# A hybrid SSM and attention layer on one core: x, B, C and z projected in row-block pairs by seven products, in a stage of their own ahead of attention

## The chip, the cores and the metric

One core of one Trainium2 chip. The metric is the device time of one execution in microseconds (us), the median of several runs. A core has five engines that run side by side, each in the order of its own instruction stream: TensorE (PE, matrix products into PSUM), VectorE (DVE), ScalarE (ACT, functions by tables), GpSimd (POOL) and SyncE (SP). In this kernel nearly every transfer is queued on SP and carried out by 16 DMA engines.

## The reference

One layer of a streaming encoder for T = 1088 columns: a prompt of 1024 positions and a running stream of 64 that has 512 cached positions. D = 1024.

```python
xn = rmsnorm(x)
z, xbc, dt, q, k, v, gate_ssm, gate_att = split(xn @ w_in)   # 2048, 3072, 32, 1024, 1024, 1024, 1024, 1024
xbc = silu(causal_dwconv(xbc, width 4) + b)                   # -> x (2048), B (512), C (512)
y = ssd_scan(x, dt, B, C) + D_skip * x                        # chunks of 64, 32 heads in 4 groups
y = rmsnorm_by_group(y * silu(z))
o = rmsnorm(softmax(q1 k1) v - lam * softmax(q2 k2) v)        # 8 heads, chunk-causal, q and k normed and rotated
mix = sigmoid(gate_ssm) * (y @ w_branch_ssm) + sigmoid(gate_att) * (o @ w_branch_attn)
x = x + mix @ w_out
ha, hb = split(rmsnorm(x) @ w_up)                             # 2816 each
x = x + (silu(causal_dwconv(ha, width 3)) * hb) @ w_down
```

Everything is float32. Outputs are the layer's result, the new keys and values, the scan's state and the last rows ahead of both convolutions.

## The kernel before

**Layout and precision.** Activations lie transposed: 128 features on the partitions, positions along the columns. A feature dimension of 1024 is eight row blocks (KT = 8). Each float32 operand is split into a high and a low part of a type that TensorE takes at full rate (`hi`, `lo`); a product is three matmuls, hi by hi, hi by lo and lo by hi (`product`, L149 to L151). A projected row block of 128 features runs over three column parts, WIDE = 384, 384, 320, with 24 matmuls for each (`project`): a *step* of the generators below. `weights` loads a block of weights, ACT makes its high part (L142) and DVE its low part (L143). `acc` hands out PSUM banks in turn.

**Order of the stages.** Front norm, from which come xn in high and low parts and the values' first half; statistics of the scan (`steps`); q; values 2 and 3; the cached keys; k. Then attention with its filler, the scan with its filler, the second half of the SSM branch, the output product with the second norm, the FFN's up-projection and its down-projection.

**Filler.** The projections of x, B and C (24 row blocks, `conv_tiles`), z (16, `z_tiles`) and the two branch gates (16, `gate_tiles`) are no stage. They are one generator, `stream`, in the order of the list ORDER, 168 steps. `fill(rate)` draws so many steps of it: ATT_STEPS = 1.9 after each attention unit, SCAN_STEPS = 1.5 at each of the scan's yields. From the fifth yield of the scan on (BRANCH_AT = 4) the generator is followed by `branch_tiles`: the attention branch (24 steps) and the first half of the SSM branch (24 steps).

**Attention.** Eight heads, nine units each (128 query positions, in the order ATT_ORDER; the last block is the stream's 64). A unit (`attend`, L510 to L586) makes two score rows of up to 1024 columns in PSUM tiles `sc`, of which there are two (L535, L536); DVE takes the maximum (L540, L544); ACT the exponential (L549); DVE the reciprocal, lambda and the difference of the two softmaxes (L551 to L553); PE transposes (L564), DVE and ACT copy (L571), PE multiplies with the values (L583). `head_out` norms a head's output (L604, L609).

**Scan.** 36 chunk steps over four groups and three column parts. It reads x, B, C (`x_sc`) and z (`z_sc`) back from memory, where the filler put them, and broadcasts decays from `a_sc`.

**Convolution and silu.** The conv block's first tap and bias are an ACT instruction (L458), three taps are DVE instructions (L460). silu is made from tanh: an ACT instruction and a DVE one (L462, L431), with the factor 0.5 folded into the parameters and the group norm's scale.

**The up-projection** already uses seven products: two row blocks by two halves of the inner dimension are one 2 x 2 block matrix, the columns in two halves the other side, and seven products of block sums take the place of eight (L992 and the lines 149 to 151 over tiles of QW = 272 columns). The weights' sums are made on GpSimd, the split into parts on ACT and DVE (L841, L842), the sums of products on DVE out of PSUM; its convolution of width 3 is L1001 and L1003.

**What sets the order.** A planner orders each engine's instructions: it holds a timeline of its own, takes what is ready by it, and among that what the program has earlier; `tc.high_priority(n)` moves an instruction ahead. The program's order above is thus a priority, not the order on the engine.

Of the kernel before, what the change touches and what calls it, by code (L numbers as in the profile page):

```python
# [12 lines left out]
ALU = mybir.AluOpType  # L13
# [52 lines left out]
ORDER = (("g", (15, 14)), ("z", range(4)), ("c", group(0)), ("g", range(13, 7, -1)), ("c", group(1)), ("c", group(2)),  # L66
         ("z", range(4, 8)), ("c", group(3)), ("z", range(8, 16)), ("g", range(7, 1, -1)))

# [7 lines left out]
def hybrid_layer(ctx: ExitStack, tc: tile.TileContext, xT, prm, cst, rope, wvd, win, wbs, wba, wout, wup, wdn,  # L76
# [9 lines left out]
    def scratch(name, shape, dt=F32):  # L86
        return dram.tile(shape, dt, name=name, tag=name)

    q_st, k_st = (scratch(n, [2 * D, T]) for n in ("q_st", "k_st"))
    c_st = scratch("c_st", [2 * D, PAST])  # L90
# [30 lines left out]
    xn_pool = tc.alloc_tile_pool(name="xn", bufs=1, side="right")  # L121

    def rows_by_part(name):

        return [[xn_pool.tile([P, KT, w], R32, name=f"{name}_{u}{x}", tag=f"{u}{x}") for u in ("hi", "lo")]
                for x, (c, w) in enumerate(WIDE)]

    xn = rows_by_part("xn")
    extra, turn, ahead, quick = None, 0, AHEAD_IN, QUICK
# [23 lines left out]
    def project(block, evac):  # L153
        w_hi, w_lo = weights(block, KT, P)
        for (c, w), (hi, lo) in zip(WIDE, xn):
            ps = acc(w)
            product(ps, [(w_hi[:, k], w_lo[:, k], hi[:, k], lo[:, k]) for k in range(KT)])
            with tc.high_priority(quick or ahead):
                evac(ps, c, w)
            yield  # L160
# [74 lines left out]
    with tc.tile_pool(name="nx", bufs=1) as nx:  # L235
        S.preload_act_table_set(LN_EXP)
        c = 0
        for x, w in enumerate(NORM):
            xc = nx.tile([P, KT, max(NORM)], F32, name="xc", tag="xc", bufs=3)
            ps = stat(w)  # L240
            for k in range(KT):
                load(out=xc[:, k, :w], in_=xT[:, k, c : c + w])
                if x == 0 and k == 3:
                    load(out=con, in_=cst)
            if x == 0:
                load(out=par, in_=prm)
                for a, b, by in ((O_MIX, O_CW, -1.0), (O_CW, O_SN, 0.5), (O_SN, O_D, -0.5), (O_QN, O_FW, -1.0)):
                    V.tensor_scalar_mul(par[:, a:b], par[:, a:b], by)
            for k in range(KT):
                sq = nx.tile([P, max(NORM)], F32, name="nsq", tag="nsq", bufs=NSQ)  # L250
                if k % 2:
                    (G if x else V).tensor_tensor(out=sq[:, :w], in0=xc[:, k, :w], in1=xc[:, k, :w], op=ALU.mult)
                else:
                    act(sq[:, :w], xc[:, k, :w], AF.Square)
                PE.matmul(ps, ones, sq[:, :w], start=k == 0, stop=k == KT - 1)
            rs = nx.tile([P, max(NORM)], F32, name="nrs", tag="nrs", bufs=2)
            rstd_of(nx, rs[:, :w], ps, w, "nn", 1.0 / D, max(NORM))
            for k in range(KT):
                xr = nx.tile([P, max(NORM)], F32, name="nxr", tag="nxr", bufs=NXR)
                (G if k % 3 == 2 else V).tensor_tensor(out=xr[:, :w], in0=xc[:, k, :w], in1=rs[:, :w], op=ALU.mult)  # L260
                hi, lo = (t[:, k, c % 384 : c % 384 + w] for t in xn[c // 384])
# [6 lines left out]

    def values(f, dt=None, pools=(None, None)):
        m = 256 if dt is None else 272  # L270
        w2 = [weights(win[B_V + 2 * f - 4 + u] if dt is None else wvd[2 * f + u], 4, m, pools[u]) for u in range(2)]
        for i in range(9):
            n = min(P, T - i * P)
            ps = acc(m)[:n]
            hi, lo = (t[:, :, P * (i % 3) : P * (i % 3) + n] for t in xn[i // 3])
            product(ps, [(hi[:, k], lo[:, k],
                          w2[k // 4][0][:, k % 4], w2[k // 4][1][:, k % 4]) for k in range(KT)])
            vo = staged("vo")[:, :256]
            with tc.high_priority(quick or ahead):
# [15 lines left out]
    with tc.tile_pool(name="qk", bufs=1) as qk:  # L295
# [113 lines left out]
        heads(B_K, lambda j: col(O_KN + j), k_st, kT)  # L409
    s1.close()  # L410
    more = None, 0
    ahead = AHEAD
    extra.release()
    extra = None
    cv_pool = tc.alloc_tile_pool(name="cv", bufs=1, side="right")

# [8 lines left out]

    def z_tiles(tiles):
        for j in tiles:
            def evac(ps, c, w):
                zr = staged("zr")[:, :w]
                act(zr, ps, AF.Tanh, scale=0.5)  # L430
                V.scalar_tensor_tensor(zr, zr, 1.0, ps, ALU.add, ALU.mult)  # L431
                load(out=z_sc[P * j : P * (j + 1), c : c + w], in_=zr)

            yield from project(win[B_Z + j], evac)

    def conv_tiles(tiles):
        for f in tiles:
            tail = None

            def evac(ps, c, w):  # L440
                nonlocal tail
                n = min(w, TP - c)
                pre = cv_pool.tile([P, 387], F32, name="pre", tag="pre", bufs=2)
                cc = cv_pool.tile([P, 384], F32, name="cc", tag="cc", bufs=3)
                if tail is None:
                    G.memset(pre[:, 0:3], 0.0)
                else:
                    G.tensor_copy(pre[:, 0:3], tail)
                S.copy(pre[:, 3 : 3 + n], ps[:, :n])
                tail, m = pre[:, n : n + 3], w  # L450
                if n < w:
                    m = w + 3
                    G.tensor_copy(pre[:, n + 3 : n + 6], par[:, O_CS + 3 * f : O_CS + 3 * f + 3])
                    S.copy(pre[:, n + 6 : w + 6], ps[:, n:])
                    G.tensor_copy(conv_o[:, f, 0:3], tail)
                    G.tensor_copy(conv_o[:, f, 3:6], pre[:, w + 3 : w + 6])
                cw = lambda i: col(O_CW + 4 * f + i)
                act(cc[:, :m], pre[:, :m], AF.Identity, bias=col(O_CB + f), scale=cw(0))  # L458
                for i in range(1, 4):
                    V.scalar_tensor_tensor(cc[:, :m], pre[:, i : i + m], cw(i), cc[:, :m], ALU.mult, ALU.add)  # L460
                act(pre[:, :m], cc[:, :m], AF.Tanh)
                V.scalar_tensor_tensor(cc[:, :m], pre[:, :m], 1.0, cc[:, :m], ALU.add, ALU.mult)  # L462
                load(out=x_sc[P * f : P * (f + 1), c : c + n], in_=cc[:, :n])
                if n < w:
                    load(out=x_sc[P * f : P * (f + 1), c + n : c + w], in_=cc[:, n + 3 : m])

            yield from project(win[B_X + f], evac)

    def stream():
        for kind, which in ORDER:  # L470
            yield from {"c": conv_tiles, "z": z_tiles, "g": gate_tiles}[kind](which)
        two = [gate_tiles([j]) for j in (1, 0)]
        for _ in WIDE:
            for u in two:
                yield next(u)
# [176 lines left out]
    with (tc.tile_pool(name="sin", bufs=1) as sin, tc.tile_pool(name="sp", bufs=1) as sp,  # L652
# [77 lines left out]
        def normed(g, c, w, xs, zt, y):  # L730
# [10 lines left out]
            load(out=part(y_sc), in_=y)  # L741

        def scan():
# [40 lines left out]
        def branch_tiles():  # L784
            nonlocal bs
            cv_pool.release()
            st.release()
            bs = tc.alloc_tile_pool(name="bs", bufs=1, side="right")
# [30 lines left out]
    bs.release()  # L819
    xn_pool.release()  # L820

# [386 lines left out]
```

## Time and profile before

| | |
|---|---|
| three runs | 2530.85, 2530.01, 2529.93 us; median 2530.01 |
| the profiled execution: span | 2526.9 us, first to last instruction |
| its own time beside the runs' | the median is 3.1 us above that span |
| PE busy | 2463.0 us (97%), 16646 matmuls |
| DVE / ACT / POOL busy | 1507.9 (60%) / 1130.1 (45%) / 522.8 us (21%) |
| DMA | 378.75 MB, 150 GB/s over the span |
| mean granted TensorE clock | 0.990 of full speed |

Rough times of the stages in the profile: q, k and values until about 390 us, attention until about 1105, the scan until about 1580, the rest of the branch and the output product until about 1770, the second norm until about 1820, the up-projection until about 2235. A busy time is the sum of an engine's instructions; PE's matmuls overlap in the pipeline, so that a matmul's own duration is longer than the distance to the next one's start.

### The profile page before, as it was taken

To read this page: it belongs to the slowest core of one execution; us is meant where nothing else is said; L and a number is where in the kernel's file an instruction comes from. 1 tells how busy PE (TensorE), PEld (TensorE's weight loads), DVE (VectorE), ACT (ScalarE), POOL (GpSimd) and SP (SyncE) were. 2 spreads that over 40 slices of the span, in tenths; PEclk is the share of its full clock that TensorE was granted. 3 is DMA by queue.
4 is the path that set the end of the run, shared out by engine and by line. 5 is a ranking of instruction groups with operands and counts; after the bars stand their busy time and mean duration, and the time that the engine had idled before them with its cause. 6 is when DMAs were issued, how large, how long until landed. Compare 5 with 4: busy or idle time off the path is not lost.

```text
span 2526.9 us, 43448 instructions
## 1 busy us (share of the span) xinstructions
PE 2463.0 (97%) x16646; PEld 2385.1 (94%) x16646; DVE 1507.9 (60%) x2597; ACT 1130.1 (45%) x2426; POOL 522.8 (21%) x584
## 2 busy tenths in 40 slices
PE   8999999999999999999999998999699999999999
PEld 8999999999999999998889898998699999999999
DVE  7326255855787677447667764645876666673422
ACT  6234343644666455357655654225443333341200
POOL 3000000100111001014333230014465555530000
PEclk9999999999999999999999999999799999999999
DMA  5217258545354344255697735663122222256553
GB/s 164 77 55 272 77 202 261 153 143 158 108 150 138 112 144 118 87 198 177 204 350 233 231 126 201 189 203 109 39 82 78 77 77 78 76 193 211 174 159 112
DMA packets 248336, 378.75 MB, mean 150 GB/s; under 512 B 31776, under 2 KB 188320, under 8 KB 248000
## 3 DMA queue, kind: packets, MB, share of 16 engines
q1 hardware_dynamic: 248128, 375.97, 46.6%
q8 instruction: 131, 2.15, 0.4%
q14 instruction: 77, 0.63, 0.1%
HBM read 254.58 MB, written 121.30 MB: 149 GB/s over the span
## 4 chain that ended last, share of the span: by engine, by line
PE 71%; DMA 4%; DVE 3%; ACT 2%; issue 1%; SPq 1%; POOL 0%; ACTq 0%; DVEq 0%; POOLq 0%
PE mx L992 12%; PE mm L149 10%; PE mm L151 10%; PE mm L150 10%; PE mm L992 5%; PE mx L151 4%; PE mx L149 4%; PE mx L150 4%; PE po L583 3%; PE sc L536 1%; PE sc L535 1%; PE pt L564 1%; PE yi L698 1%; PE ye L704 1%; DMA bc<-a_sc 1%; PE stp L710 1%
## 5 line engine op out<-in xcount | busy, mean ns | idle before, releaser
L149 PE MATMUL mm<-xn_hi,w_hi 128*128 128x384 f32 (+1 forms) x1416 | 469.8, 332 | 0.9 <-DVE zr L431 0.9
L151 PE MATMUL mm<-xn_hi,w_lo 128*128 128x384 f32 (+1 forms) x1416 | 467.7, 330 | 0.4 <-DVE w_lo L143 0.4
L150 PE MATMUL mm<-xn_lo,w_hi 128*128 128x384 f32 (+1 forms) x1416 | 466.5, 329 | 0.0
L142 ACT CAST w_hi<-w_f 128x1024 fp32r<-128x1024 f32 (+2 forms) x144 | 149.3, 1037 | 308.1 <-PE mx L150 162.2
L149 PEld LDWEIGHTS mm<-xn_hi,w_hi 128*128 128x128 f32 x1416 | 266.2, 188 | 5.3 <-issue 2.0
L151 PEld LDWEIGHTS mm<-xn_hi,w_lo 128*128 128x128 f32 x1416 | 266.1, 188 | 2.9 <-issue 0.8
L150 PEld LDWEIGHTS mm<-xn_lo,w_hi 128*128 128x128 f32 x1416 | 266.2, 188 | 1.8 <-issue 0.6
L143 DVE TENSOR_TENSOR w_lo<-w_f,w_hi 128x1024 fp32r<-128x1024 f32 (+2 forms) x144 | 181.2, 1259 | 133.4 <-ACT w_hi L142 133.0
L149 PE MATMUL mm<-b_hi,w_hi 128*128 128x384 f32 (+1 forms) x448 | 148.2, 332 | 7.6 <-DVE b_g L193 4.4
L151 PE MATMUL mm<-b_hi,w_lo 128*128 128x384 f32 (+1 forms) x448 | 147.0, 328 | 0.0
L150 PE MATMUL mm<-b_lo,w_hi 128*128 128x384 f32 (+1 forms) x448 | 146.9, 328 | 0.0
L992 PE MATMUL mx<-n,wh 128*128 128x272 f32 x752 | 143.4, 289 | 1.4 <-ACT wh L841 1.4
L992 PE MATMUL mx<-m,w_hi 128*128 128x272 f32 x752 | 142.7, 288 | 0.0
L460 DVE SCALAR_TENSOR_TENSOR cc<-pre,par,cc 128x384 f32<-128x384 f32 (+1 forms) x216 | 126.6, 586 | 23.8 <-ACT cc L458 18.7
L549 ACT ACTIVATE p_t<-sc,mx 128x1024 f32<-128x1024 f32 (+5 forms) x144 | 106.1, 739 | 74.6 <-DVE mx L540 37.1
L992 PEld LDWEIGHTS mx<-n,wh 128*128 128x128 f32 x752 | 118.3, 189 | 1.7 <-ACT wh L841 1.7
L992 PEld LDWEIGHTS mx<-m,w_hi 128*128 128x128 f32 x752 | 118.1, 188 | 0.0
L1009 POOL TENSOR_TENSOR hb<-hb,cc 128x544 f32<-128x544 f32 (+2 forms) x66 | 88.4, 1353 | 115.1 <-ACT w_hi L841 95.0
L151 PE MATMUL mx<-m,w_lo 128*128 128x272 f32 (+2 forms) x366 | 111.9, 307 | 0.0
L150 PE MATMUL mx<-m,w_hi 128*128 128x272 f32 (+2 forms) x366 | 111.9, 306 | 0.0
L149 PE MATMUL mx<-m,w_hi 128*128 128x272 f32 (+2 forms) x366 | 111.8, 306 | 0.0
L992 PE MATMUL mx<-m,w_lo 128*128 128x272 f32 x376 | 108.4, 288 | 0.0
(339 smaller groups left out, 6595.4 us busy)
## 6 DMA issues: line engine op xcount, KB each, us to landing
w_f<-in_win_dram SPq DMA_DIRECT2D x76, 512.0 KB, 3.8
w_f<-in_wup_dram SPq DMA_DIRECT2D x44, 512.0 KB, 3.5
bc<-a_sc SPq DMA_DIRECT2D x32, 512.0 KB, 6.1
h_sc<-hb SPq DMA_DIRECT2D x44, 272.0 KB, 2.1
hr<-h_sc SPq DMA_DIRECT2D x44, 272.0 KB, 5.2
x_sc<-cc SPq DMA_DIRECT2D x48, 192.0 KB, 2.2
xa<-x_sc SPq DMA_DIRECT2D x48, 192.0 KB, 2.5
kh_t<-k_st SPq DMA_DIRECT2D x32, 272.0 KB, 7.5
```

The costliest lines, as they stand in the source:

```text
L142: S.copy(hi, w)
L143: V.tensor_tensor(out=lo, in0=w, in1=hi, op=ALU.subtract)
L149: PE.matmul(ps, a_hi, b_hi, start=i == 0, stop=False)
L150: PE.matmul(ps, a_hi, b_lo, start=False, stop=False)
L151: PE.matmul(ps, a_lo, b_hi, start=False, stop=i == n - 1)
L460: V.scalar_tensor_tensor(cc[:, :m], pre[:, i : i + m], cw(i), cc[:, :m], ALU.mult, ALU.add)
L535: PE.matmul(ps[:n, a : a + b], lhs, r_hi, start=True, stop=False)
L536: PE.matmul(ps[:n, a : a + b], lhs, r_lo, start=False, stop=True)
L549: act(p_t[:n, :nk], sc[c][:n, :nk], AF.Exp, bias=mx[:n, c : c + 1], accum_out=dst)
L583: PE.matmul(po[:n, :P], a_t[b // 4][:kw, b % 4 * P : b % 4 * P + n], rhs, start=b == 0, stop=b == nb - 1)
L992: PE.matmul(ps, w[x][:, c], b[y][:, k], start=start and k == i == 0, stop=k == 3 and i == 2, skip_group_check=not start)
L1009: G.tensor_tensor(out=hb[h][:, o : o + n], in0=hb[h][:, o : o + n], in1=cc[:, d : d + n], op=ALU.mult)
```

## The change

A new stage stands between k and attention. In it, 12 pairs of conv row blocks and 8 pairs of z row blocks (PAIRS: conv, z, conv, conv, z, four times over) are each made by seven products over tiles of 272 columns. For this

- xn is one tile of 1088 columns for each part, and no longer one for each column part; the four sums of its quarters that the seven products need (`differences`) are made by DVE, GpSimd and ACT, the last of them in the place of a quarter of xn that goes to memory (`b_sc`) and comes back at the last pair;
- values 2 and 3 move from before the cached keys to the place beside those sums;
- six more PSUM banks serve the stage;
- `Gated` and `Conv` take the sums out of PSUM; a convolution works on half the columns at a time (544, or 547 with the stream), and silu is ACT's own function, so that the DVE instruction behind it and the factors of 0.5 go.

`stream`, ORDER, `z_tiles`, `conv_tiles` and BRANCH_AT are gone. The filler is the 16 gate blocks (48 steps): six steps ahead of attention, 0.53 for each unit, and then, from the scan's first yield on, at 1.08 a yield, what is left of them, the attention branch and the first half of the SSM branch, which waits for the scan's first group. The branch's input tiles get a pool of their own (`bx`) in xn's place once the gates are done.

```diff
-ATT_STEPS = 1.9
-SCAN_STEPS = 1.5
-BRANCH_AT = 4
+GATES_AHEAD = 6
+ATT_STEPS = 0.53
+SCAN_STEPS = 1.08
...
+PAIRS = [p for i in range(4) for p in (("c", CONV[6 * i], CONV[6 * i + 1]), ("z", 4 * i, 4 * i + 1),
+                                       ("c", CONV[6 * i + 2], CONV[6 * i + 3]),
+                                       ("c", CONV[6 * i + 4], CONV[6 * i + 5]), ("z", 4 * i + 2, 4 * i + 3))]
...
-                for a, b, by in ((O_MIX, O_CW, -1.0), (O_CW, O_SN, 0.5), (O_SN, O_D, -0.5), (O_QN, O_FW, -1.0)):
+                for a, b, by in ((O_MIX, O_CW, -1.0), (O_SN, O_D, -1.0), (O_QN, O_FW, -1.0)):
...
         heads(B_Q, lambda j: wq8[:, j : j + 1], q_st, None)
-        run(values(2))
-        run(values(3))
...
+    def left_blocks(b0, b1, row):
+        a = []
+        for b in (b0, b1):
+            w = wp.tile([P, WMAX], F32, name="w_f", tag="w_f", bufs=2)
+            load(out=w[:, :1024], in_=b)
+            a += [w[:, :512], w[:, 512:1024]]
...
+        G.tensor_tensor(out=s1, in0=q21, in1=q22, op=ALU.add)
+        G.tensor_tensor(out=s2, in0=s1, in1=q11, op=ALU.subtract)
...
+    for u in range(2):
+        for k in range(4):
+            load(out=b_sc[P * u : P * (u + 1), T // 2 * k : T // 2 * (k + 1)], in_=xn[u][:, k, T // 2 :].bitcast(F32))
...
+    for s in range(2):
+        for j in range(2):
+            differences(s, j, late)
+    for f in (2, 3):
+        run(values(f, out=lambda n: mrow("fu", n)))
...
+    class Gated(Rows):
...
+            if u is None:
+                act(t, ps, AF.Silu)
+            else:
+                V.tensor_tensor(out=t, in0=ps, in1=u[:, s], op=ALU.add)
...
+        def convolve(self, r, h):
...
+            act(cc, t[:, :n], AF.Identity, bias=col(O_CB + f), scale=cw(0))
+            for i in range(1, 4):
+                V.scalar_tensor_tensor(cc, t[:, i : i + n], cw(i), cc, ALU.mult, ALU.add)
+            act(cc, cc, AF.Silu)
...
+            for k in range(4):
+                c = slice(P * k, P * (k + 1))
+                for i, (x, y) in enumerate(((0, 0), (0, 1), (1, 0))):
+                    PE.matmul(ps, w[x][:, c], b[y][:, k], start=start and k == i == 0, stop=k == 3 and i == 2,
+                              skip_group_check=not start)
...
+    for n, at in enumerate(PAIRS):
+        coming = blocks_of(*PAIRS[n + 1]) if n + 1 < len(PAIRS) else iter(())
...
+            if n + 1 == len(PAIRS) and (p, s) == (4, 1):
+                for x in range(2):
+                    for k in range(4):
+                        load(out=xn[x][:, k, T // 2 :].bitcast(F32), in_=b_sc[P * x : P * (x + 1), T // 2 * k : T // 2 * (k + 1)])
...
-    filler, spare = stream(), 0.0
+    filler, spare = gate_tiles(range(15, -1, -1)), 0.0
...
+    fill(GATES_AHEAD)
...
-            rstd_of(sp, rs, rs, w, "gn", 0.25 / 512)
+            rstd_of(sp, rs, rs, w, "gn", 1.0 / 512)
...
+            while ready.count(1) < len(WIDE):
+                yield
             yield from branch(stage, side, y_sc[:D], wbs[0], None, (), store(n_sc))
-        bs, late = None, chain(filler, branch_tiles())
+        bs, filler = None, chain(filler, branch_tiles())
         for i in scan():
-            if i == BRANCH_AT and late is not None:
-                filler, late = late, None
             fill(SCAN_STEPS)
```

More of the change, by code (lines that the diff above doesn't have):

```diff
@@ L409, in hybrid_layer, with half, quarter, split @@
         heads(B_K, lambda j: col(O_KN + j), k_st, kT)
-    s1.close()
-    more = None, 0
-    ahead = AHEAD
     extra.release()
     extra = None
-    cv_pool = tc.alloc_tile_pool(name="cv", bufs=1, side="right")
+    st.release()
+    def half(h):
+        return slice(0, 4) if h == 0 else slice(4, 8)
+    def quarter(kh, q):
+        return [t[:, half(kh), QW * q : QW * (q + 1)] for t in xn]
+    def split(hi, lo, src):
+        S.copy(hi, src)
+        V.tensor_tensor(out=lo, in0=src, in1=hi, op=ALU.subtract)
@@ new lines, in hybrid_layer, with __init__, at @@
+    late = []
+    for s in range(2):
+        for j in range(2):
+            differences(s, j, late)
+    for f in (2, 3):
+        run(values(f, out=lambda n: mrow("fu", n)))
+    for src, s, js in late:
+        hi, lo = X["t1", s]
+        split(hi[:, js], lo[:, js], src)
+    s1.close()
+    psb = ExitStack()
+    more = psb.enter_context(tc.tile_pool(name="psb", bufs=6, space=PSUM)), 6
+    ahead = AHEAD
+    class Rows:
+        def __init__(self, f, g):
+            self.f = (f, g)
+            self.t = {}
+            self.u1, self.u2 = (couple(mrow("fu", n)) for n in ("u1", "u2"))
+        def at(self, r, h):
+            if (r, h) not in self.t:
+                self.t[r, h] = mrow("pr", "pre")
+                self.made(r, h)
+            return self.t[r, h]
@@ new lines, in blocks_of @@
+    def blocks_of(kind, f, g):
+        b = B_X if kind == "c" else B_Z
+        return left_blocks(win[b + f], win[b + g], mrow)
+    both = [(p, s) for p in range(7) for s in range(2)]
+    early, rest = [(p, s) for p in (0, 2) for s in range(2)], [(p, s) for p in (1, 3, 4, 5, 6) for s in range(2)]
+    left = list(blocks_of(*PAIRS[0]))
+    for n, at in enumerate(PAIRS):
+        coming = blocks_of(*PAIRS[n + 1]) if n + 1 < len(PAIRS) else iter(())
+        nxt = []
+        u = seven(*at, left)
+        next(u)
+        for p, s in (early + rest if n == 0 else both):
+            u.send((p, s))
+            if s == 1:
+                nxt += [x for x in [next(coming, None)] if x is not None]
+            if n + 1 == len(PAIRS) and (p, s) == (4, 1):
+                for x in range(2):
+                    for k in range(4):
+                        load(out=xn[x][:, k, T // 2 :].bitcast(F32), in_=b_sc[P * x : P * (x + 1), T // 2 * k : T // 2 * (k + 1)])
+        left = nxt + list(coming)
@@ L424, in gate_tiles @@
             yield from project(win[B_G + j], evac)
[L426 to L467, printed above, removed]
```

163 lines of the change are left out of this document (143 added, 20 removed).

## The prediction

> **What bounds the kernel now.** I read the page first, then the windows by stage, then single instructions of TensorE (PE) and VectorE (DVE).
>
> ```profile
> span 2526.9 us, 43448 instructions
> PE 2463.0 (97%) x16646; PEld 2385.1 (94%) x16646; DVE 1507.9 (60%) x2597; ACT 1130.1 (45%) x2426; POOL 522.8 (21%) x584
> PE   8999999999999999999999998999699999999999
> GB/s 164 77 55 272 77 202 261 153 143 158 108 150 138 112 144 118 87 198 177 204 350 233 231 126 201 189 203 109 39 82 78 77 77 78 76 193 211 174 159 112
> ```
>
> PE is busy 97% of the span, all but three of the 40 slices are full: nothing is gained except by less PE work, and PE work that is taken away is all gain only while what remains still covers the other engines. The windows are attention with its filler, scan with its filler, the scan's end, and the up-projection, which already uses seven products.
>
> ```profile
> 475.00:1105.00 630.00, 628.61 (x4046) 606.03 (x4045) 415.97 (x903) 335.70 (x841) 43.50 (x124) 1.00 0.45 134
> 1105.00:1545.00 440.00, 428.77 (x2907) 388.73 (x2906) 289.16 (x365) 266.58 (x585) 157.26 (x104) 0.99 0.66 211
> 1545.00:1580.00 35.00, 27.36 (x140) 26.68 (x139) 18.76 (x36) 16.61 (x34) 0.00 (x0) 0.86 0.78 266
> 1820.00:2235.00 415.00, 415.00 (x3311) 415.00 (x3310) 287.60 (x441) 165.26 (x296) 224.70 (x239) 1.00 0.24 79
> ```
>
> Columns: length, busy PE, weight load, DVE, ScalarE (ACT), GpSimd (POOL), granted clock, DMA share, GB/s. Attention leaves PE idle for 1.4 us of 630, the scan 11.2 of 440, because row blocks of the projection lie beside every head and chunk. The up-projection shows that seven products can run with PE never idle.
>
> **The removed and added matmuls.** 40 row blocks (24 conv, 16 z), each 24 matmuls in each of three column parts, become 20 pairs of 168 matmuls of 272 columns. By the instruction order of the changed kernel, 1920 matmuls of 384 columns and 960 of 320 go, 3360 of 272 come; so "the change doesn't do what it says" is excluded. A matmul costs its pitch, from start to start:
>
> ```profile
> 640.11 0.34 PE L149 MATMUL mm<-xn_hi,w_hi 128*128 128x384 f32 x1
> ...
> 641.67 0.31 PE L149 MATMUL mm<-xn_hi,w_hi 128*128 128x320 f32 x1
> ...
> 643.57 0.28 PE L535 MATMUL sc<-kh_t,q_t 128*128 128x256 f32 x1
> ...
> 1859.60 1.50 PE mm L992 x12
> ```
>
> Nine matmuls of 384 columns take 641.67 - 640.11 = 1.56 us, 0.1735 each; thirteen of 320 take 1.90, 0.1467 each; twelve of 272 in the up-projection take 1.50, 0.1254 each (the last row is from the chain that ended last). So 1920 x 0.1735 + 960 x 0.1467 = 473.9 us go and 3360 x 0.1254 = 421.3 come: **-52.6 us**. Those 473.9 us, however, were what covered attention and the scan, and the 421.3 now stand alone ahead of them.
>
> **Attention without cover.** The only filler left is 16 gate blocks in 48 steps of 24 matmuls, a step 24 x (2 x 0.1735 + 0.1467)/3 = 3.95 us. Six are drawn ahead of attention, the rest at 0.53 a unit (8 heads of 9 units). But what an engine runs next is the planner's choice, and the instruction order of the changed kernel shows that PE has taken the last gate matmul after 33.5 of the 72 units, as a waiting unit lets the next ready matmul past; after it come 38.5 units, 4.3 heads, with nothing beside them. What does a bare head cost? The groups of instructions by line (count after the x, busy us and mean ns after the bar, idle time before them last) give PE's share, then DVE's:
>
> ```profile
> L583 PE MATMUL po<-v_t,a_t 128*128 128x128 f32 x576 | 78.6, 274 | 0.0
> L564 PE MATMUL pt<-con,p_t 128*128 128x128 f32 x288 | 46.3, 274 | 0.9 <-DVE p_t L553 0.9
> L535 PE MATMUL sc<-kh_t,q_t 128*128 128x512 f32 x96 | 39.4, 410 | 0.1
> 862.18 1.34 PE po L583 x12
> L540 DVE TENSOR_REDUCE mx<-sc 128x1 f32<-128x1024 f32 (+4 forms) x80 | 76.5, 963 | 18.0 <-PE sc L536 17.1
> L553 DVE SCALAR_TENSOR_TENSOR p_t<-p_t,sm 128x1024 f32<-128x1024 f32 (+8 forms) x72 | 58.4, 812 | 1.9
> L571 DVE COPY a_t<-pt 128x512 f32<-128x512 f32 (+3 forms) x56 | 29.9, 534 | 21.0 <-PE pt L564 20.7
> L544 DVE TENSOR_REDUCE mx<-sc 128x2 f32<-128x256 f32 (+3 forms) x32 | 26.2, 817 | 0.4
> L604 DVE SCALAR_TENSOR_TENSOR o_t<-o_t,ors,wsub 128x128 f32<-128x128 f32 (+1 forms) x72 | 19.4, 341 | 0.1
> L552 DVE SCALAR_TENSOR_TENSOR sm<-sm,nlam,s 128x1 f32<-128x1 f32 (+1 forms) x72 | 15.2, 212 | 1.5
> L609 DVE TENSOR_TENSOR ol<-pt,oh 128x512 fp32r<-128x512 f32 (+1 forms) x24 | 12.2, 525 | 5.5 <-ACT gt L421 4.5 <-DMA o_sc<-ol 0.8 <-ACT oh L608 0.2
> L551 DVE RECIPROCAL sm<-sm 128x1 f32<-128x1 f32 (+1 forms) x72 | 11.4, 158 | 29.3 <-ACT p_t L549 28.8
> ```
>
> PE: a head has 56 score matmuls of 20,736 columns together, at 0.1735/384 a column 9.4 us; 50 transposes and 82 products with the values, 132 at 1.34/12 = 0.112, 14.8; together 24.2 us. DVE: the eight rows sum to 249.2 us, 31.1 a head. So bare, DVE binds, not PE, and 31 us a head is the floor. The ceiling comes from the chain inside one unit:
>
> ```profile
> 804.12 0.49 PE L535 MATMUL sc<-kh_t,q_t 128*128 128x512 f32 x1
> ...
> 805.54 1.23 DVE L540 TENSOR_REDUCE mx<-sc 128x1 f32<-128x1024 f32 x1
> ...
> 811.21 1.28 DVE L553 SCALAR_TENSOR_TENSOR p_t<-p_t,sm 128x1024 f32<-128x1024 f32 x1
> ```
>
> From the first score matmul to the end of the softmax a wide unit takes 811.21 + 1.28 - 804.12 = 8.4 us (other work lies in it); transposes and value products follow. The score banks allow some two units in flight, so nine units take 9 x 8.4 = 76 us in sequence, and some 53 if neighbours overlap by 30%. Between 31 and 53 I take 42, the middle, as five of nine units are wide and fill both score buffers. Net of PE's own share: 4.29 heads x (42 - 24.2) = **+76 us** (31: +30; 53: +124). The covered 3.7 heads cost PE as before: a unit has 2.7 us of its own and 1.25 steps of 3.95, against some 3.5 of DVE.
>
> **The new stage.** Does DVE keep up with 21.07 us a pair (168 x 0.1254)? The up-projection's 415 us are 415/21.07 = 19.7 pairs, at 287.60/19.7 = 14.6 us of DVE each. A conv pair here differs by its filter: 12 additions of some 545 columns where the up-projection has four.
>
> ```profile
> L1003 DVE SCALAR_TENSOR_TENSOR cc<-pre,par,cc 128x544 f32<-128x544 f32 (+1 forms) x88 | 81.5, 926 | 9.2 <-ACT cc L1001 7.7
> L460 DVE SCALAR_TENSOR_TENSOR cc<-pre,par,cc 128x384 f32<-128x384 f32 (+1 forms) x216 | 126.6, 586 | 23.8 <-ACT cc L458 18.7 <-POOL pre L448 2.4 <-DMA x_sc<-cc 0.3
> ```
>
> At 0.926: 14.6 + 8 x 0.926 = 22.0 us for a conv pair, above PE's 21.07; a z pair has no filter, 14.6 - 3.7 = 10.9. Twenty pairs: 12 x 22.0 + 8 x 10.9 = 351 of 421 us. The z pairs between let DVE catch up, as the planner has a pair's buffers to spare: 0 to +28 (that end by 23.4 us a conv pair, a filter addition at 1.04 us as the slower half of that row's instructions had, nothing caught up), taken **+6**. The silu by its function drops two DVE operations a tile and adds none: nothing on the path.
>
> The row at L1003 (0.926 us for 545 columns, with POOL busy 224.70 of 415 us) against L460 (0.586 for 384, which by columns makes 0.83) shows what GpSimd beside it costs DVE, some 11%. The Trainium skill, page "SBUF — State Buffer", section "Who interferes with whom", says that a DVE instruction with two SBUF inputs contends with a GpSimd instruction that reads SBUF. By it the stage, whose five weight sums a pair are GpSimd's as well, keeps the dear price; were it the cheap one, a conv pair would be 21.3 us and the term about +3.
>
> **The edges.** Two changeovers are new. Into the stage: K's finish, its stores and the differences of xn on DVE, covered by the values moved there (18 products x 24 x 0.125 = 54 us of PE). Out of it: half of xn comes back from memory by eight DMAs (2.2 MB), queued on SP with the last z stores, the gate weights and head 0's loads, and covered by the six gate steps, 24 us; 2.2 MB are 6 us at the busiest slice's 350 GB/s. If the cover fails, PE waits. The nearest row is the changeover that exists, 1545 to 1580: 7.6 us of PE idle. Each edge: 0 to +15 (twice that), taken +5, **+10** together. The spill's eight stores stand early on SP, and nothing waits for them but the write over xn's place.
>
> **The scan.** Its filler is now the 48 steps of two branches. PE is 456 us busy over 1105 to 1580; without conv, z and gate blocks I count some 320. The transfers stay: 0.66 x 440 = 290 us of DMA share would be 0.9 of 320, and in the row where the share was 0.78 PE was idle 22%. DVE, 289.16 before with filters in it, is no tighter. From 0 (the scan hides it as before) to +40, taken **+15**, nearer the low end, as a share of 0.66 cost only 11.2 us in 440.
>
> **Sum.** Around the span of 2526.9 lie 3.1 us to the median 2530.0 (runs 2529.9 to 2530.9). 2530.0 - 52.6 + 76 + 6 + 10 + 15 = **2584 us**.
>
> **Rivals.**
> First, *attention at DVE's floor* (ends faster). The planner packs bare units until DVE is full: 33 us a head, +38; with stage, edges and scan at +5 in all it gives 2530.0 - 52.6 + 38 + 5 = **2520**. The point where it decides: with the other terms at +5 the change gains below 24.2 + 47.6/4.29 = 35 us a bare head; with them at the +31 taken, below 29, under the floor. For it: PE's queue already mixes units freely. Against: DVE waited 18 us at L540 and 29 at L551 even with filler about.
>
> Second, *the clock falls in bare attention*. PE is then 24.2 of 42 us busy. The rows of the norm ahead of the up-projection show what gaps do:
>
> ```profile
> 1770.00:1775.00 5.00, 0.00 (x0) 0.00 (x0) 5.00 (x7) 2.58 (x5) 3.87 (x3) 0.50 0.01 2
> 1785.00:1790.00 5.00, 3.99 (x19) 3.77 (x17) 5.00 (x6) 2.67 (x5) 3.53 (x3) 0.63 0.01 3
> 1810.00:1815.00 5.00, 3.56 (x29) 3.35 (x28) 2.60 (x4) 2.92 (x5) 2.64 (x3) 1.00 0.04 9
> ```
>
> The eighth column is the granted clock: 0.50 where PE stood still, 0.63 soon after, yet 1.00 at 3.56 busy of 5. At half clock a head's 24.2 us are 48.4; with waits 55: 4.29 x 30.8 = +132, in all **2640**. Against it: bare attention's gaps should be a microsecond or two. The Trainium skill, page "TensorE: Matmul & The Clock Gate", section "HAM oscillation — how this bites in real kernels", has the clock fall after PE idles some 3.4 us; by that rule, which these rows agree with (0.50 after idling, 1.00 in dense use with small gaps), it decides only if a unit's wait outlasts that.
>
> Third, *DVE binds the new stage*: +28 instead of +6, **2606**. For it: 22.0 against 21.07; against: eight z pairs at half the load.
>
> **The numbers.** Forecast 0.48 (2584), floor 0.23 (2520), clock 0.15 (2640), stage 0.14 (2606). The range runs from 2507 (31 us a bare head, the other terms at nothing) to 2645 (the clock rival) and leaves a tenth at each end. About 0.2% (5 us) is what a measurement of this kernel tells from no change: faster 0.23 (the floor rival), same 0.04 (cut from the forecast's lower tail), slower 0.73. As sign and size hang on the bare heads, the likeliest case's own range is 2555 to 2625.
>
> **What would show it.** Right: stage of some 425 us with PE full; the first half of attention full; then a stretch of about 180 us with PE some 60% busy and DVE near 75%, clock near 1. Floor rival: that stretch 140 us, DVE over 90%. Clock rival: granted clock well under 0.9 there. Stage rival: PE idle on DVE in conv pairs. The prediction is wrong if gate matmuls still lie beside the last heads, or if PE idles over 20 us at either edge.

## The result and the profile after

The changed kernel takes 2709.7 us (median of four runs, 2708.0 to 2711.2) against 2530.4 for the kernel before on the same chip (2529.9 to 2531.1): a ratio of 1.071, 95% interval 1.070 to 1.073. It is slower by 179 us, where 54 were forecast and 2645 was the range's upper end.

The page of the changed kernel, with the lines that answer to those of before:

```profile
span 2706.2 us, 44595 instructions
PE 2461.8 (91%) x17126; PEld 2360.7 (87%) x17126; DVE 1652.7 (61%) x2764; ACT 1157.4 (43%) x2453; POOL 681.3 (25%) x652
PE   8996759999999999877688899699789999999999
PEclk9998879999999999887899999899889999999999
```

Two things are to be read from these four lines. PE is idle for 2706.2 - 2461.8 = 244.4 us, where before it was 63.9: 180.5 us more, which by this count is the whole slowdown (the spans differ by 179.3). And PE is as busy as before (2461.8 against 2463.0) although 52.6 us of matmuls were saved: the matmuls that are left take longer, at a lower clock (mean 0.958 against 0.990). The slices that lost their nines are the fourth to sixth, the seventeenth to twenty-third, and the twenty-sixth, at the scan's end; the twenty-ninth and thirtieth are the second norm, which was thin before as well.

Windows of the changed kernel by stretch (length, busy PE, weight load, DVE, ACT, POOL, clock, DMA share, GB/s): the changeover from q to k, the one behind k, the new stage, the way out of it, attention with gates, attention without, the scan, the scan's end.

```profile
200.00:235.00 35.00, 11.47 (x60) 11.15 (x60) 24.44 (x30) 14.40 (x23) 0.00 (x0) 0.66 0.86 331
320.00:400.00 80.00, 34.46 (x249) 33.71 (x248) 57.84 (x60) 21.40 (x36) 31.37 (x20) 0.70 0.48 183
408.00:831.00 423.00, 423.00 (x3365) 421.77 (x3364) 323.23 (x506) 190.03 (x339) 164.64 (x192) 1.00 0.31 104
831.00:847.00 16.00, 16.00 (x98) 16.00 (x97) 4.26 (x14) 5.45 (x9) 0.00 (x0) 1.00 0.94 307
847.00:1120.00 273.00, 269.10 (x1740) 256.72 (x1739) 142.35 (x316) 125.78 (x338) 0.00 (x0) 1.00 0.53 155
1120.00:1319.00 199.00, 145.62 (x816) 120.24 (x816) 128.38 (x335) 106.18 (x320) 0.00 (x0) 0.83 0.41 113
1319.00:1732.00 413.00, 351.68 (x2359) 303.32 (x2358) 288.66 (x372) 252.62 (x566) 167.09 (x104) 0.95 0.68 219
1732.00:1842.00 110.00, 93.80 (x559) 93.41 (x558) 69.10 (x143) 31.34 (x74) 0.00 (x0) 0.92 0.56 178
```

The same stretches of the kernel before, as far as the prediction's windows do not show them: both changeovers, all of attention, the scan, its end.

```profile
200.00:235.00 35.00, 35.00 (x296) 35.00 (x295) 23.45 (x25) 13.01 (x21) 0.00 (x0) 1.00 0.86 315
320.00:400.00 80.00, 78.63 (x467) 76.83 (x466) 45.03 (x61) 32.35 (x49) 0.10 (x1) 1.00 0.62 235
410.00:1087.00 677.00, 674.38 (x4329) 648.66 (x4328) 460.16 (x991) 365.93 (x923) 48.36 (x143) 1.00 0.46 135
1087.00:1534.00 447.00, 435.77 (x2960) 395.42 (x2959) 293.30 (x380) 268.68 (x591) 157.26 (x104) 0.99 0.68 217
1534.00:1664.00 130.00, 122.36 (x716) 121.52 (x715) 76.78 (x154) 41.75 (x92) 0.00 (x0) 0.96 0.59 189
```

Length less busy PE is what PE idled; busy time times (1 - clock) estimates what the clock added to it. What each stretch lost, before and after:

| stretch | idle before | idle after | more idle | more by the clock (estimate) | forecast |
|---|---|---|---|---|---|
| q to k, and behind k | 1.4 | 69.1 | 67.7 | 14 | +5 |
| the new stage | - | 0.0 | 0 | 0 | +6 |
| attention | 2.6 | 57.3 | 54.7 | 25 | +76 |
| scan | 11.2 | 61.3 | 50.1 | 13 | +15 |
| scan's end | 7.6 | 16.2 | 8.6 | 3 | (with the scan) |
| out of the stage | - | 0 | 0 | 0 | +5 |

The losses sum to 236 us; with the 52.6 saved that makes 184, against 179 measured. Attention comes to 80 where 76 were forecast, though 25 of the 80 are clock, which the forecast did not have. In the new stage PE is never idle: 423.00 busy of 423.00. Nearly all of the miss lies in the first row (82 us where 5 were given) and in the scan (some 75 with its end, where 15 were given).

What PE waited for between 200 and 400 us (engine, line, what released it; us in total, times, longest):

```profile
PE mx L156 <- ACT vo L287: 34.2, 2, 30.1
PE mm L156 <- ACT ss L330: 23.5, 1, 23.5
PE mx L156 <- ACT w_hi L149: 11.3, 1, 11.3
```

The 23.5 us are k's first block, which waits for the row `ss`: it needs one of ten row buffers (QR = 10), which q fills until it has been normed and stored. Values 2 and 3 stood there before, and 35.00 of 35.00 us were busy. The 30.1 us are the moved values themselves: their output tiles `vo` lie in the stage's pool, in the place of k's rows, so that after the PSUM banks are full they wait for k's stores. The first line shows it: the copy of the first `vo` out of PSUM starts when a store of k's low part (`k_st<-ql`) is done, and PE starts 0.4 us later. The other lines are from the chain that ended last: the same store releases the differences of xn on DVE and GpSimd.

```profile
350.59 0.37 ACT L287 COPY vo<-mx 128x256 f32<-128x256 f32 x1 [8.60 <-DMA k_st<-ql]
...
347.72 2.69 DMA k_st<-ql
350.73 0.78 DVE xf L486 x2
...
372.75 6.70 POOL xf L499
```

The last line is one sum on GpSimd that takes 6.7 us; PE stands for another 4 us behind it, as ACT's next copies come after it.

### The profile page after: what moved, and what is told of

It reads as the page before. It is cut to its first block, busy times and chain, and to the rows that moved or that the text cites. A ratio compares the mean times of both kernels' runs of the same rounds, so it can differ in the third digit from the quotient of the medians.

```text
span 2706.2 us, 44595 instructions
## 1 busy us (share of the span) xinstructions
PE 2461.8 (91%) x17126; PEld 2360.7 (87%) x17126; DVE 1652.7 (61%) x2764; ACT 1157.4 (43%) x2453; POOL 681.3 (25%) x652
## 4 chain that ended last, share of the span: by engine, by line
PE 71%; DVE 10%; DMA 7%; ACT 6%; issue 3%; SPq 2%; POOL 1%; DVEq 0%; ACTq 0%; POOLq 0%
PE mx L1182 11%; PE mx L603 11%; PE mm L156 6%; PE mm L157 6%; PE mm L158 6%; PE mx L158 5%; PE mx L156 5%; PE mx L157 5%; PE mm L603 5%; PE mm L1182 5%; PE po L769 2%; DMA kl_t<-k_st 2%; PE sc L722 1%; PE sc L721 1%; ACT bc L875 1%
## 5 line engine op out<-in xcount | busy, mean ns | idle before, releaser
L149 ACT CAST w_hi<-w_f 128x1024 fp32r<-128x1024 f32 (+2 forms) x104 | 107.3, 1033 | 273.0 <-PE mx L157 175.4
L156 PE MATMUL mm<-xn_hi,w_hi 128*128 128x384 f32 (+1 forms) x528 | 175.0, 332 | 23.5 <-ACT ss L330 23.5
L150 DVE TENSOR_TENSOR w_lo<-w_f,w_hi 128x1024 fp32r<-128x1024 f32 (+2 forms) x104 | 134.9, 1298 | 71.7 <-ACT w_hi L149 71.2
L156 PE MATMUL mm<-b_hi,w_hi 128*128 128x384 f32 (+1 forms) x448 | 154.6, 346 | 23.5 <-DVE b_g L200 16.2
L158 PE MATMUL mm<-xn_hi,w_lo 128*128 128x384 f32 (+1 forms) x528 | 175.9, 333 | 0.0
L157 PE MATMUL mm<-xn_lo,w_hi 128*128 128x384 f32 (+1 forms) x528 | 175.1, 332 | 0.0
L585 DVE SCALAR_TENSOR_TENSOR cc<-pre,par,cc 128x544 f32<-128x544 f32 (+1 forms) x144 | 131.7, 941 | 0.4
L156 PEld LDWEIGHTS mm<-xn_hi,w_hi 128*128 128x128 f32 x528 | 100.0, 189 | 24.6 <-ACT ss L330 23.8
L156 PEld LDWEIGHTS mm<-b_hi,w_hi 128*128 128x128 f32 x448 | 86.5, 193 | 30.5 <-issue 20.8
L1182 PE MATMUL mx<-n,wl 128*128 128x272 f32 x376 | 108.9, 291 | 0.4 <-DVE wl L1032 0.4
L157 PE MATMUL mx<-m,w_hi 128*128 128x272 f32 (+2 forms) x356 | 109.1, 307 | 0.0
```

The costliest lines, as they stand in the source:

```text
L149: S.copy(hi, w)
L150: V.tensor_tensor(out=lo, in0=w, in1=hi, op=ALU.subtract)
L156: PE.matmul(ps, a_hi, b_hi, start=i == 0, stop=False)
L157: PE.matmul(ps, a_hi, b_lo, start=False, stop=False)
L158: PE.matmul(ps, a_lo, b_hi, start=False, stop=i == n - 1)
L585: V.scalar_tensor_tensor(cc, t[:, i : i + n], cw(i), cc, ALU.mult, ALU.add)
```

## Experiments

All start from the changed kernel unless they say otherwise; times are medians beside runs of the kernel before on the same chip (2527 to 2531 us).

**Values back in their old place.**

```diff
         heads(B_Q, lambda j: wq8[:, j : j + 1], q_st, None)
+        run(values(2))
+        run(values(3))
...
-    for f in (2, 3):
-        run(values(f, out=lambda n: mrow("fu", n)))
```

> The changed kernel with values 2 and 3 back between q and the cached keys, nothing else. Theory 1 (two changeovers, one cover: the q changeover lacks it now, and the k changeover lasts as long as its own chain of DVE work, stores and differences, some 86 us, whatever PE does in it): the 31 us idle near 200 to 235 us are filled by 52 us of values, the k changeover stays near 86 us with hardly any PE work in it, in all about 2710 + 20 = 2730 us. Rival (the k changeover lasts because the values are in its way): it shrinks by what the values took, 52 us, and the q stall goes, about 2680 us.

Measured: 2717.2 us (ratio to before 1.075, 1.072 to 1.078), some 7 slower than the changed kernel; the interval touches that one's (1.070 to 1.073), so that no more is shown than that it is not faster. Windows: the changeover from q to k, and the one behind k.

```profile
200.00:235.00 35.00, 35.00 (x297) 35.00 (x295) 22.70 (x25) 13.57 (x21) 0.00 (x0) 1.00 0.87 319
320.00:420.00 100.00, 30.58 (x160) 27.59 (x160) 73.53 (x77) 28.44 (x46) 35.15 (x20) 0.64 0.36 143
```

The first is full again; the second now idles 69 us of 100. PE's last projection of k ends at about 330 us and the stage runs densely from about 425, some 95 us; with the values in it, it was 305 to 408, 103 us. So taking 52 us of values away from this changeover shortens it by little, and the rival falls: it lasts by its own chain. There are two changeovers, and the values can cover one.

**Gates behind k.** Values back as above, and 18 gate steps drawn between k and the stage.

```diff
+    ahead = AHEAD
+    fill(18)
...
-ZR = 3
+ZR = 2
-MID = dict(fa=8, fs=2, fu=4, pr=6, cc=4)
+MID = dict(fa=8, fs=2, fu=4, pr=6, cc=3)
```

> The changed kernel with values 2 and 3 back between q and the cached keys, and 18 of the gate steps between k and the new stage (their output tiles kept there, which costs the stage one convolution row and one row of z's staging). Theory 1 (the changeover behind k lasts some 85 us by its own chain and has room for 71 us of gate matmuls; both changeovers are then covered): as the run with the values back, 2717, less what 18 steps cost beside attention (full price, 71, where they stand in covered heads, less the bare time they leave behind: about 2.6 us a step, 47): about 2670 us. Rival (the changeover grows by what is put into it): 2717 us or more.

Measured: 2691.4 us (1.064, 1.061 to 1.067), 18 less than the changed kernel, where 40 were expected. Windows: behind k, and all of attention.

```profile
320.00:440.00 120.00, 106.31 (x628) 103.86 (x627) 85.76 (x84) 47.87 (x77) 35.06 (x24) 0.94 0.45 171
866.00:1308.00 442.00, 363.75 (x2175) 321.74 (x2174) 260.99 (x644) 219.05 (x634) 0.00 (x0) 0.90 0.53 149
```

Both changeovers are now covered, with 14 us idle of 120 behind k. The rows that the stage gives up for it (ZR, `cc`) cost it 2 us of idle time. But attention, 18 gate steps poorer, is only 30 us shorter (442 against 472 from 847 to 1319) for 381 matmuls fewer, some 63 us at 0.164 each, the mean of a step, and idles 78 us in place of 57. A step moved is missed where it was.

**All gates ahead of attention.**

```diff
-GATES_AHEAD = 6
+GATES_AHEAD = 48
```

> The changed kernel with all 48 gate steps drawn ahead of attention, so that all eight heads stand bare; measures the bare head. Theory 2 (a bare head costs some 48 us by the chain through the score banks): eight heads take about 384 us, 42 steps more stand ahead (+166 us), the 3.7 heads that were covered in 261 us take 178; about 2710 + 83 = 2793 us. Rival (a bare head at the VectorE floor of 31 to 35 us, the slow stretch of the changed kernel being the last heads' own trouble): eight heads in 265 us, about 2675 us.

Measured: 2777.1 us (1.099, 1.095 to 1.103). The window from the last gates to attention's end:

```profile
1022.00:1394.00 372.00, 275.73 (x1547) 229.96 (x1546) 238.75 (x619) 194.93 (x587) 0.00 (x0) 0.83 0.50 138
```

Eight nearly bare heads take 372 us, 46.5 each, with DVE at 64%: the forecast's 42 was near, and the floor rival (33) falls. What PE waited for there:

```profile
PE sc L721 <- ACT p_t L735: 43.0, 29, 3.3
PE sc L721 <- DMA kh_t<-k_st: 12.0, 5, 3.3
PE pt L750 <- DVE ol L795: 9.5, 7, 2.2
```

Of 96 us idle, 43 are score matmuls that wait for a score bank, which the exponential frees.

**Dummies.** All gates ahead, and six more matmuls of 512 columns in every unit, whose result nothing reads.

```diff
                 fill(ATT_STEPS)
+                ps = acc(512)
+                for d in range(6):
+                    PE.matmul(ps, tiles[0][0][:, :P], tiles[1][0][:, :512], start=d == 0, stop=d == 5)
```

> As the run with all gates ahead, with six more matmuls of 512 columns in each unit, whose result nothing reads (1.4 us of TensorE a unit, 12.7 a head). They cost nothing if TensorE waits for a chain; they keep its clock up. Theory 2 with the chain alone: the time of the run with all gates ahead, within 10 us, at a clock near 1. Rival 1 (the low clock makes the bare heads long): 20 to 40 us faster than that run. Rival 2 (TensorE binds): 100 us slower.

Measured: 2800.7 us (1.108, 1.105 to 1.111), 24 more than without them. The same stretch:

```profile
1022.00:1420.00 398.00, 346.69 (x1969) 289.65 (x1968) 243.33 (x617) 193.97 (x585) 0.00 (x0) 0.92 0.47 128
```

Of 8 x 12.7 = 101 us of matmuls, 26 show in the whole stretch, and none of the three expectations held to the number. But the planner had not spread the dummies evenly: 162 of the 432 stand ahead of the third head, where 18 of the 26 us arise, and none beside the last. The four whole heads from the third to the sixth (from one head's first reciprocal to that of a later one), without dummies and with them:

```profile
1106.80:1300.00 193.20, 141.04 (x776) 117.07 (x776) 124.85 (x328) 102.07 (x308) 0.00 (x0) 0.81 0.57 155
1125.10:1322.20 197.10, 169.66 (x968) 139.87 (x968) 126.93 (x328) 100.76 (x305) 0.00 (x0) 0.93 0.55 152
```

There four heads have 216 dummies beside them, some 51 us, and last 3.9 us longer (49.3 us a head against 48.3). That is the chain theory's sign: these matmuls are nearly free beside it. The clock rose from 0.81 to 0.93 and the heads did not get shorter, as they would have if the low clock made them long and the dummies cost nothing. What the dummies cost and what the clock gave back are not told apart here, only their sum, 1 us a head.

**Gates pinned to their units**, by block and by step: a one-column copy of the unit's output goes into the weight tile before its load, or into the step's PSUM bank before its matmuls.

```diff
+        if pin is not None:
+            V.tensor_copy(w[:TS, 0:1], pin)
...
+                    pin = o_t[:TS, ATT_ORDER[x - 1], 0:1]
```

> The changed kernel, where each gate block's weights may load only after the attention unit behind which the program draws them (one tiny copy of a column of that unit's output into the weight tile, ahead of the load), so that the gates lie beside all eight heads. Theory 2: each head takes some 50 us with 24 us of its own and about 20 of gates in it, 400 us in place of 466, and some steps are left for the changeover to the scan: about 2640 us. Rival (attention's loss is not for want of cover, since the same matmuls are there): 2710 us.

```diff
             ps = acc(w)
+            if pin is not None:
+                V.tensor_copy(ps[:TS, 0:1], pin)
```

> As the run with pinned gates, but each step of 24 matmuls waits for its attention unit (a one-column copy of that unit's output into the step's PSUM bank ahead of its matmuls), and the weights load freely. Theory 2b (a bare head is 47 us of chain with 24 of TensorE in it; gates in lumps of 72 matmuls fill it for 12 us and leave it bare for 45, single steps fill it evenly): 8 heads of 50 to 52 us in place of 57, some 40 us faster than the pinned gates, about 2660 us. Rival (gate matmuls lengthen the chain wherever they stand, as TensorE takes them in order with the scores): no faster than the pinned gates, 2700 us.

Measured: 2700.2 us (1.069, 1.065 to 1.072) and 2704.9 us (1.069, 1.066 to 1.072), 10 and 5 less than the changed kernel, where 70 and 50 were expected; both intervals overlap the changed kernel's. All of attention in the first and in the second:

```profile
854.00:1325.00 471.00, 401.04 (x2400) 356.65 (x2399) 266.85 (x662) 228.65 (x650) 0.00 (x0) 0.91 0.45 129
847.00:1317.00 470.00, 409.63 (x2487) 366.68 (x2486) 272.34 (x686) 228.76 (x651) 0.00 (x0) 0.92 0.47 133
```

With the changed kernel's 472 that is the same length in all three arrangements. Counted by the windows' matmuls against the bare window's 1547, the first has 36 steps more, 36 x 3.95 = 142 us, and is 99 us longer; the second 39 steps, 154 us, and 98; the changed kernel 42 steps, 166 us, and 100. So a gate matmul hides 30 to 40% of itself, by blocks, by steps, or all in the first heads. It is not that the gates lie in the wrong heads, as the forecast had it; there are too few of them, and what there is hides poorly. Why a step of 24 matmuls hides less than six dummies do (30 to 40% against 75%) is open. That a step holds PE for 4 us ahead of a score matmul is one guess; another is that a gate brings work for the chain's own engines, its weights' parts and its output (the first of these windows has 28 us more of DVE and 34 more of ACT than the bare one, the dummies' 5 and none). No run here tests either.

**The scan alone.** The branch steps that stood beside it wait for its last output.

```diff
-SCAN_STEPS = 1.08
+SCAN_STEPS = 0
...
+        pin = last_y[0][:TS, 0, 0:1]
         run(filler)
```

> The changed kernel with nothing beside the scan: the branch steps that were drawn beside it (48, and one gate block) are drawn behind it, their weights waiting for the scan's last output. Measures the bare scan. Theory 3 (the scan lasts by its own chain through VectorE, ScalarE, GpSimd and the transfers, so that cover taken out of it does not shorten it): the scan takes 350 to 390 us in place of 413 although 200 us of TensorE work are gone from it, and the whole 2710 - 413 + 365 + 220 = 2880 us. Rival 1 (the branch's transfers and VectorE work are what slows the scan): the scan takes 290 us, the whole about 2805. Rival 2 (TensorE's order binds it): 230 us, the whole about 2745.

Measured: 2857.3 us (1.130, 1.127 to 1.132). The scan's window:

```profile
1308.00:1643.00 335.00, 208.09 (x1196) 138.43 (x1197) 231.68 (x294) 213.69 (x493) 153.45 (x104) 0.72 0.51 155
```

335 us with nothing beside it: 15 under what the chain theory gave, 45 over the nearer of its rivals. No engine is full (DVE 69%, ACT 64%), and the transfers are at 0.51. The waits between 1340 and 1640 us go round:

```profile
POOL bc L875 <- ACT e L862: 60.9, 16, 16.0
ACT grs L925 <- PE gst L922: 35.2, 7, 8.4
...
PE cb L867 <- ACT b_cb L870: 26.5, 11, 6.5
POOL state L903 <- DVE state L905: 23.0, 9, 4.2
DVE bc L878 <- ACT b_cb L870: 22.9, 6, 6.8
```

So the scan is a chain over four engines, of 335 us at the clock of 0.72 that PE had in it. Beside it, the changed kernel puts 2359 - 1196 = 1163 more matmuls, some 191 us at 0.164, and takes 413: 78 us of them, 41%, show. The kernel before lies on the same line, with 1764 matmuls more, 289 us, and 447 us: 112 us of them, 39%, show.

**z back beside attention.** Only conv pairs in the stage; z as 48 plain steps of the filler.

```diff
+PAIRS = [p for p in PAIRS if p[0] == "c"]
-ATT_STEPS = 0.53
+ATT_STEPS = 1.15
...
-    filler, spare = gate_tiles(range(15, -1, -1)), 0.0
+    filler, spare = chain(z_tiles(range(16)), gate_tiles(range(15, -1, -1))), 0.0
```

> Part of the change alone: the stage makes the 12 conv pairs only; z is projected by plain products in 48 steps of the filler ahead of the gates, at 1.15 steps a unit, with silu of z by tanh as before. Theory 2 (cover is what attention lacks): eight pairs of 21.1 us go from the stage (-169), 48 steps come (+190), attention has no bare head any more (24.2 x 8 + 89 x 3.95 = 546 us from the gates ahead to its end, where the changed kernel takes 485 for 41 steps fewer), and some steps cover the changeover to the scan (-20): about 2610 us. Rival (the seven products themselves are what counts): 2710 + 21 = 2731 us.

Measured: 2650.2 us (1.048, 1.045 to 1.051), 60 less than the changed kernel though it spends 8 x 2.6 = 21 us more on matmuls, and 40 more than the theory gave; the rival (2731) falls. Attention and the scan:

```profile
685.00:1261.00 576.00, 565.35 (x3651) 537.72 (x3651) 314.34 (x710) 265.98 (x719) 0.00 (x0) 1.00 0.48 140
1261.00:1665.00 404.00, 351.85 (x2351) 302.69 (x2350) 293.88 (x362) 248.55 (x556) 166.75 (x104) 0.95 0.68 217
```

Attention is full again (565 of 576, clock 1.00). The scan is nearly what it was, 404 us with 52 idle, 9 us shorter where 20 were expected.

**Both**: z in the filler and 18 of its steps behind k, values back; the first lines are against the run before.

```diff
-ATT_STEPS = 1.15
+ATT_STEPS = 0.95
...
+    fill(18)
```

> The last two changes together: only conv pairs in the stage, z in the filler (at 0.95 steps a unit), values back between q and the cached keys, 18 steps of filler (here z) between k and the stage. Theory (each stretch that lacks cover costs by itself): the run with z beside attention, 2650, less the 70 us of waiting that covered changeovers save, plus 18 that the stage's start takes back, plus some 20 because the last heads are left bare: about 2615 us. Rival (the filler is one stock, and what is taken from attention is missed there in full): 2650 us.

Measured: 2646.3 us (1.046, 1.044 to 1.048): the rival, and within the noise the time of the run before. Windows: behind k, and all of attention.

```profile
320.00:435.00 115.00, 87.97 (x515) 86.11 (x514) 82.43 (x96) 44.57 (x71) 26.51 (x20) 0.91 0.46 172
714.00:1258.00 544.00, 510.42 (x3231) 477.92 (x3231) 298.88 (x685) 253.68 (x696) 0.00 (x0) 0.97 0.48 138
```

Behind k it idles 27 us of 115, and attention idles 34 where the run before had 11; 25 of these lie after 1150 us, at its end, where the steps are missing. These two are the fastest of all and still far behind the kernel before; no run here points to a version that beats it.

**Differences of xn on VectorE alone.**

```diff
-        f12, f11 = whole("pr", 0, 2 + s, V), whole("fa", 0, s, G)
+        f12, f11 = whole("pr", 0, 2 + s, V), whole("fa", 0, s, V)
...
-        G.tensor_tensor(out=f12, in0=f22, in1=f12, op=ALU.subtract)
+        V.tensor_tensor(out=f12, in0=f22, in1=f12, op=ALU.subtract)
...
-        f21 = whole("cc", 1, s, G)
+        f21 = whole("cc", 1, s, V)
```

> The changed kernel with GpSimd's three sums in each part of the differences of xn moved to VectorE. In the changed kernel these sums take 1.8 us on GpSimd and slow VectorE's next to them from 0.7 to 1.9 us. Theory 4 (the two hold each other up): VectorE has 12 more sums of 0.65 us but all at the short time, and the changeover shortens by 6 to 10 us: 2701 us. Rival (VectorE is the chain's bound there, and takes 8 us more): 2717 us.

Measured: 2699.7 us (1.067, 1.066 to 1.069; four runs), 10 less than the changed kernel and 1.3 from what theory 4 gave. The sums of xn between 350 and 400 us, in this run and then in the changed kernel on DVE and on POOL:

```profile
L486 DVE TENSOR_TENSOR xf<-xn_hi,xn_lo 128x544 f32<-128x544 f32 x16 | 10.7, 718 | 3.0 <-DMA k_st<-ql 3.0
```

```profile
L486 DVE TENSOR_TENSOR xf<-xn_hi,xn_lo 128x544 f32<-128x544 f32 x8 | 11.1, 1439 | 3.0 <-DMA k_st<-ql 3.0
L486 POOL TENSOR_TENSOR xf<-xn_hi,xn_lo 128x544 f32<-128x544 f32 x8 | 14.0, 1766 | 295.0 <-DMA k_st<-ql 294.1 <-ACT w_hi L149 0.9
```

Sixteen sums on DVE alone take less time (10.7 us) than eight beside GpSimd (11.1).

## Why the prediction was wrong

*The matmuls saved* were right: the stage does 20 pairs in 423 us, where 421.3 were counted, and PE is never idle in it.

*Attention without cover* was right in sign and size, +76 against some 80, and its bare head (42) near the measured 46.5. The 43 us of waits for a score bank bear out its chain. That the head came so near is in part luck, as 42 was the middle of two bounds, 31 and 53, and was not worked out. Its picture of the cause was not quite right: pinning showed that it hardly matters which heads are left bare.

*The new stage* was given 6 and cost nothing; the stage rival fell, with DVE at 76% there (323.23 of 423.00, where the text counted 351). A filter addition took 0.941 us, as dear as priced; GpSimd makes four weight sums a pair there (L441, L442, L452, L459) and not the text's five.

*The edges* are the step that failed. The text priced the changeover behind k by the nearest row, 7.6 us, and took +5 with the moved values as its cover; its own sign of being wrong, over 20 us idle at an edge, came with 45.5 of 80 us. It named what the values would newly cover and did not ask what they had covered: the changeover from q to k, which lost 23.5 us in one wait. And behind k it counted 54 us of values as cover without asking where their output lies: in the place of k's rows. Measured, the two changeovers together lost 68 us idle and some 14 by the clock. The run with the values back and the one with gates behind k show both halves. The edge out of the stage, given 5, cost nothing.

*The scan* is the second step that failed, mis-sized: +15, measured some 75 with its end. The text took the scan for PE work plus a little idle, and bounded it by its DMA share. The bare scan takes 335 us by its chain, more than the 320 us of PE work that the text counted, and work beside it adds only some 40% of itself. So the cover taken away (2960 - 2359 = 601 matmuls by the two windows, some 99 us) shortened it only by 34 (447 to 413), and 65 of the 99 us went to waits and to the clock.

*The rivals.* The floor rival fell at 46.5 us a bare head. The clock rival's sign came, 0.83 in the bare heads where the forecast had near 1, but not its price: 46.5 us a head and not 55, and in the run with dummies a clock of 0.93 in place of 0.81 did not shorten four whole heads. The Trainium skill, page "TensorE: Matmul & The Clock Gate", section "HAM oscillation — how this bites in real kernels", ties the lower clock to idle gaps over some 3.4 us; the waits in the eight bare heads are at most 3.3 us each and the mean clock there is 0.83, so in this case shorter gaps lower it as well. In one place of that run the clock halves after 11.8 us in which PE's longest wait is 1.9:

```profile
1136.00:1147.80 11.80, 9.50 (x63) 7.50 (x62) 9.80 (x26) 6.55 (x23) 0.00 (x0) 1.00 0.71 176
1147.80:1154.60 6.80, 5.34 (x22) 4.53 (x22) 1.42 (x3) 2.33 (x7) 0.00 (x0) 0.50 1.04 285
```

*Not run apart* are the change's other edits, silu by its own function, xn as one tile and the stage's PSUM banks; the stage that they serve shows no idle time.

## What to carry to other kernels

Work that fills other engines' waits is not removed by being made cheaper: before a filler is turned into a stage, measure every stretch that it covers bare (here 46.5 us a head and 335 us the scan), since a saving of 53 us stood against 181 us of new idle time and some 55 by the clock. A piece of work that is moved to cover a wait has to be asked two things: what it covered where it stood, and whether its own outputs wait for the very thing that it is to cover. And a stretch full of waits shows a lower clock too; before that is counted as a price of its own, matmuls that nothing reads can be put beside the chain, as here, where the clock rose and the heads stayed as long.

## What the hardware showed beyond that

Sums of two SBUF tiles of 128x544 took 0.718 us on DVE alone and 1.439 in the mean beside GpSimd's own sums (1.766 each), twice as long, where the prediction took 11% from the filters; with GpSimd's share on DVE all sixteen were done sooner. The Trainium skill, page "SBUF — State Buffer", section "Who interferes with whom", has just these two kinds of instruction contend, and the run agrees. PE's busy time did not fall by the 52.6 us of matmuls saved, as the granted clock fell from 0.990 to 0.958 in the mean; the table's estimate of what that added is 55 us.
